# RWKV columns of a hybrid backbone layer: low-rank products ahead of the norm's sums, bonus operands ahead of both directions' work

## The chip, the cores and the metric

The kernel runs on one core of a Trainium2 chip. The metric is the device time of one execution in microseconds (us); lower is better. The engines of the core work side by side, each through its own instructions in order: TensorE (PE, with its weight loads PEld), VectorE (DVE), ScalarE (ACT), GpSimd (POOL), and SyncE (SP), which here only issues DMAs. ACT issues DMAs too.

## The reference, cut to what matters

One layer of a diffusion backbone over 256 context and 2048 latent tokens (2304 in all). After a modulated norm, one input projection feeds two head groups; the change lies in the preparation of the second, eight heads of two-directional RWKV-7 mixing with 64 channels each:

```python
u = _dwconv(z[..., 3 * ATT_WIDTH:], w_ts)          # width-3 shift over tokens
r, kr, v = ...                                     # 512 columns of u each
xw, xa, xg = ...                                   # 2x64, 2x64 and 128 columns
w_log = -softplus(-(w0 + einsum('btnl,nlc->btnc', tanh(xw), w2))) - 0.5
decay = exp(-exp(w_log))
a = sigmoid(a0 + einsum('btnl,nlc->btnc', xa, a2))
g = sigmoid(xg) @ g2
kk = heads(kr * k_k)
kk = kk * rsqrt(sum(kk * kk, -1) + 1e-12)          # the norm, per head
kd = kr[:, :, None] * (1.0 + (a - 1.0) * k_a)      # per direction
S_f, y_f = _wkv_scan(..., kk, kk * a_f, v, kd_f); S_b, y_b = _wkv_scan(..., kk, kk * a_b, v, kd_b, reverse)
y = groupnorm(y_f + y_b) * ln_g + ln_b
bonus = sum(sum(r * kd * r_k, -1) * v, directions)
out = (y + bonus) * g
```

Attention, the output projection, the gated MLP with its convolution and the final norm follow; the change doesn't touch them.

## The kernel before, in words

The program runs in stages: the input projection with attention's columns, then `rwkv_columns`, then attention, the scan, the output projection and the MLP. This case is about `rwkv_columns`.

Tokens go in three blocks of 768 (b = 2, 1, 0). In a block, three projections make the inputs of the low-rank products (`lora`), and then each of four head pairs p (128 columns, two heads) takes three: `kr`, `r` and `v`. A projection is one `gemm`: 48 matmuls (line 55) over eight chunks of the model width, three terms of high and low parts, two halves of columns in two PSUM tiles `g`. `conv3` (lines 114 and 116) takes a pair of such tiles out of PSUM: ACT writes the middle tap, DVE adds the two others. There are two tiles of each name `g`, so a gemm waits for the `conv3` of the gemm two ahead of it. For each gemm, ACT rounds a weight tile to its high part (`wh`, line 36), and POOL subtracts it for the low part (`wl`, line 46).

What is left of a pair is the generator `rest`. Its steps run during the *next* pair's three gemms: `gemm3` calls `tick` after each of the eight chunks, so 24 steps are there. Each `yield` ends a step. In order of `rest`:

- the squares of `kr` and their parts `sh`, `sl` (ACT squares and rounds, DVE subtracts, line 46);
- **the norm**: per half of the tokens a product of `bones` (ones for each head) with `sh` and `sl` (line 823), its root on ACT (line 841), then on DVE the reciprocal (line 843) and `kk` (line 844);
- **eight low-rank products** of three matmuls (line 823), for two directions, two kinds (`w2`, `a2`) and two halves; each is followed by a Tanh on ACT (line 853), each whole tile by a scale on DVE (line 855);
- `v` transposed, and sent out;
- `ms` (ACT, line 871), the bonus weights `t0` (DVE, lines 874, 876, 877);
- **the directions**: for each a scan over the decay's logarithm (DVE, line 883), two exponentials on ACT (lines 886 and 888), and products that make `ar` and `bk`: on POOL `a` times `kk`, `kr` times `m`, `r` times `e1` (lines 892, 895, 898), on DVE lines 893, 896 and 897. `ar` and `bk` have one buffer each and leave by DMA (line 900);
- **the bonus operands** `th`, `tl`, the high and low part of `t0`, in the buffers `sh` and `sl` (ACT line 36, DVE line 46), then an empty step;
- the bonus's product of `bones` with `th` and `tl`, which DVE multiplies by `v` (line 913), and the gate's product (ACT line 916, DVE line 917), per half. All products share three PSUM tiles `lr`.

The order written here is not quite the order on an engine: a scheduler ahead of the compiler sorts each engine's instructions by its own estimates, within what the data allow. So the rows of each engine's order are shown below where they matter. When the last pair's rest has run out, attention begins; its loads stand behind the last `g` writes (line 921) in SP's queue.

Of the kernel before, what the change touches and what calls it, by code (L numbers as in the profile page):

```python
# [7 lines left out]
F32 = mybir.dt.float32  # L8
F32R = mybir.dt.float32r
BF16 = mybir.dt.bfloat16  # L10
F16 = mybir.dt.float16
AF = mybir.ActivationFunctionType
ALU = mybir.AluOpType
# [9 lines left out]
BLK = 768  # L23
# [19 lines left out]
def split(hi_eng, lo_eng, hi, lo, src):  # L43

    copy(hi_eng, hi, src)
    lo_eng.tensor_sub(lo, src, hi)  # L46
# [761 lines left out]
def rwkv_columns(tc, ident, consts, R, h, window, gemm):  # L808


    nc = tc.nc
    with tc.tile_pool(name="i1", bufs=1) as i1, tc.tile_pool(name="i2", bufs=2) as i2, tc.tile_pool(
        name="ip", bufs=2, space=PSUM
# [4 lines left out]
        def product(st, x, s):  # L818

            ps = ip.tile([128, 512], F32, name="lr", bufs=3)  # L820
            terms = [(st[0], x[0]), (st[1], x[0]), (st[0], x[1])] if len(st) == 2 else [(st[0], x[0]), (st[0], x[1])]
            for i, (A, B) in enumerate(terms):
                nc.tensor.matmul(ps[:, :384], A, B[:, s], start=i == 0, stop=i == len(terms) - 1)
            return ps[:, :384]

        HALVES = [slice(q * 384, q * 384 + 384) for q in range(2)]

        def rest(b, p, kr, r, v, lora):
# [4 lines left out]
            sh = i2.tile([128, BLK], F32R, name="sh", bufs=1)  # L833
            sl = i2.tile([128, BLK], F32R, name="sl", bufs=1)
            split(nc.scalar, nc.vector, sh, sl, sq)
            for _ in range(3):
                yield
            kk = i2.tile([128, BLK], F32, name="kk", bufs=1)
            nrm = i2.tile([128, BLK], F32, name="sq", bufs=1)
            for s in HALVES:  # L840
                nc.scalar.activation(nrm[:, s], product((bones,), (sh, sl), s), AF.Sqrt, bias=tiny)
                yield
            nc.vector.reciprocal(nrm, nrm)
            nc.vector.scalar_tensor_tensor(kk, kr, col["k_k"][:, pc], nrm, op0=ALU.mult, op1=ALU.mult)
            lr = []
            for n in range(2):
                rows = slice(n * 64, n * 64 + 64)
                for w, x, bias in (("w2", lora[0], col[f"w0{n}"]), ("a2", lora[1], col[f"a0{n}"])):

                    t = i2.tile([128, BLK], F32, name=w)  # L850
                    for s in HALVES:
                        ps = product([z[rows, p, :] for z in lw[w]], [z[rows] for z in x], s)
                        nc.scalar.activation(t[:, s], ps, AF.Tanh, scale=0.5, bias=bias[:, pc])
                        yield
                    nc.vector.tensor_scalar(t, t, 0.5, 0.5, op0=ALU.mult, op1=ALU.add)
                    lr.append(t)
            vt = i2.tile([128, 6, 128], F32, name="vt", bufs=1)
            for t in range(0, 6, 3):
                tp = ip.tile([128, 512], F32, name="aux", bufs=1)
# [15 lines left out]
            mm = i2.tile([128, BLK], F32, name="sl", bufs=1)  # L875
            nc.vector.tensor_add(mm, ms[0], ms[1])
            nc.vector.tensor_mul(t0, t0, mm)
            for n in range(2):
                sg, a = lr[2 * n : 2 * n + 2]
                m = ms[n]  # L880
                cs = i2.tile([128, BLK], F32, name="t1")
                rev = (lambda t: t) if n == 0 else (lambda t: t[:, ::-1])
                nc.vector.tensor_tensor_scan(rev(cs), rev(cmask[n]), rev(sg), 0.0, ALU.mult, ALU.add)
                e1 = decay[n]
                lo = 1 - n
                nc.scalar.activation(e1[:, :, lo : lo + 64], ch(cs), AF.Exp, scale=-CW)
                e2 = i2.tile([128, BLK], F32, name="e2", bufs=1)
                nc.scalar.activation(e2, cs, AF.Exp, scale=CW)
                nc.gpsimd.tensor_copy(R["pc"][:, n, b * 12 : b * 12 + 12, p], e1[:, :, 64 * (1 - n)])
                ar = i2.tile([128, 12, 2, 64], F32, name="ar", bufs=1)  # L890
                bk = i2.tile([128, 12, 2, 64], F32, name="bk", bufs=1)
                nc.gpsimd.tensor_mul(a, kk, a)
                nc.vector.scalar_tensor_tensor(bk[:, :, 0, :], ch(a), -1.0, ch(e2), op0=ALU.mult, op1=ALU.mult)
                kd = i2.tile([128, BLK], F32, name="t1")
                nc.gpsimd.tensor_mul(kd, kr, m)
                nc.vector.tensor_mul(bk[:, :, 1, :], ch(kd), ch(e2))
                nc.vector.tensor_mul(ar[:, :, 0, :], ch(kk), e1[:, :, n : n + 64])
                nc.gpsimd.tensor_mul(ar[:, :, 1, :], ch(r), e1[:, :, lo : lo + 64])
                for nm, t in (("ar", ar), ("bk", bk)):
                    nc.sync.dma_start(  # L900
                        R[nm][n, b * 12 : b * 12 + 12, :, p, :].rearrange("c p s -> p c s"),
                        t.rearrange("p c x t -> p c (x t)"),
                    )
                yield
            th = i2.tile([128, BLK], F32R, name="sh", bufs=1)
            tl = i2.tile([128, BLK], F32R, name="sl", bufs=1)
            split(nc.scalar, nc.vector, th, tl, t0)
            yield
            yield
            g1 = i2.tile([128, BLK], F32, name="m0", bufs=1)  # L910
            g2 = i2.tile([128, BLK], F32, name="m1", bufs=1)
            for s in HALVES:
# [661 lines left out]
```

## Time and profile before

| | us |
|---|---|
| median of 3 runs (4527.21 to 4528.01) | 4527.84 |
| profiled execution, its time | 4528.56 |
| profiled execution, its span | 4526.8 |
| PE busy, share of the span | 3852.0, 85% |
| DVE busy | 3115.0, 69% |
| POOL busy | 2323.6, 51% |
| ACT busy | 1845.9, 41% |

The span is the time from the first to the last instruction of the profiled execution. Busy shares are means over all stages; `rwkv_columns` takes some 620 us of the span, from about 560 to 1180 us, and is read by itself below.

### The profile page before, as it was taken

Reading aid. Unit: us, or ns where it says so; the run is one execution under the profiler, and the core shown is the slowest. Engines: PE = TensorE matmul, PEld = TensorE weight load, DVE = VectorE, ACT = ScalarE, POOL = GpSimd, SP = SyncE. Lnnn points to the kernel's source line nnn. Section 1 sums busy time; section 2 is a strip of 40 time slices with the busy share of each in tenths; the row PEclk is TensorE's granted clock in tenths of the full one; section 3 lists DMA queues with packets and bytes.
Section 4 is the critical chain, followed back from the end, with each engine's and each line's share of the span. In section 5 each row is a group of like instructions: output and inputs, shape, how many; then the busy total and the mean of one; then the engine's idle time right before and its main releaser. Section 6 shows DMA issues by size and latency. Waiting matters only on the chain. (4 is left out here: it accounts for less than half of the span.)

```text
span 4526.8 us, 78134 instructions
## 1 busy us (share of the span) xinstructions
PE 3852.0 (85%) x29954; PEld 3414.9 (75%) x29954; DVE 3115.0 (69%) x4658; ACT 1845.9 (41%) x3728; POOL 2323.6 (51%) x1879
## 2 busy tenths in 40 slices
PE   6798987888388887899886886999988999889996
PEld 6787877777266666788775665888877999779995
DVE  4325586868577774566664224888888888878887
ACT  2421254544377773455442223333334333343332
POOL 0334344545234336555664444666656776667662
PEclk9899998989599997999998997999988999999998
DMA  5787545453756623323343443221223222232222
GB/s 211 243 280 212 145 117 165 114 159 112 178 116 135 128 58 102 86 76 81 95 102 105 167 149 94 61 66 61 66 80 112 68 64 70 84 106 63 70 70 66
DMA packets 682387, 513.24 MB, mean 113 GB/s; under 512 B 234691, under 2 KB 612612, under 8 KB 677916
## 3 DMA queue, kind: packets, MB, share of 16 engines
q1 hardware_dynamic: 508444, 378.64, 30.0%
q10 hardware_dynamic: 170080, 118.06, 8.8%
q0 software_dynamic: 3488, 11.54, 0.8%
q8 instruction: 236, 3.87, 0.4%
q14 instruction: 139, 1.14, 0.1%
HBM read 369.85 MB, written 139.76 MB: 113 GB/s over the span
## 5 line engine op out<-in xcount | busy, mean ns | idle before, releaser
L46 POOL TENSOR_TENSOR wl<-wr,wh 128x512 fp32r<-128x512 f32 (+1 forms) x349 | 613.2, 1758 | 575.3 <-ACT wh L36 503.8
L55 PE MATMUL g<-h,wh 128*128 128x384 f32 (+1 forms) x2592 | 641.8, 359 | 32.3 <-DVE r L116 8.4
L36 ACT ACTIVATE wh<-wr 128x512 fp32r<-128x512 f32 (+1 forms) x485 | 336.3, 704 | 500.2 <-DMA wr<-in_w_ffn_dram 210.1
L55 PEld LDWEIGHTS g<-h,wh 128*128 128x128 f32 x2592 | 487.6, 200 | 67.1 <-issue 27.7
L507 DVE TENSOR_TENSOR yacc<-yacc,yp 128x512 f32<-128x512 f32 x756 | 479.3, 680 | 28.9 <-PE yp L499 5.2
L456 PE MATMUL u<-hT,wh 128*128 128x386 f32 x1056 | 366.8, 347 | 38.3 <-DVE st L465 24.8
L456 PE MATMUL u<-lT,wh 128*128 128x386 f32 x1056 | 364.4, 345 | 12.2 <-DVE lT L46 12.2
L456 PE MATMUL u<-hT,wl 128*128 128x386 f32 x1056 | 364.4, 345 | 3.8 <-POOL wl L46 3.8
L55 PE MATMUL g<-h,wl 128*128 128x384 f32 (+1 forms) x1296 | 359.9, 355 | 0.0
L499 PE MATMUL yp<-w2h,gh 128*128 128x512 f32 x792 | 273.1, 418 | 48.6 <-DVE yacc L507 20.0
L46 DVE TENSOR_TENSOR wl<-wr,wh 128x512 fp32r<-128x512 f32 (+1 forms) x136 | 251.9, 1853 | 63.2 <-ACT wh L36 63.1
L456 PE MATMUL u<-h,wh 128*128 128x386 f32 x792 | 272.7, 344 | 19.3 <-ACT h L36 17.5
L456 PE MATMUL u<-l,wh 128*128 128x386 f32 x792 | 271.7, 345 | 8.2 <-DVE l L46 7.9
L456 PE MATMUL u<-h,wl 128*128 128x386 f32 x792 | 274.4, 346 | 0.0
L499 PE MATMUL yp<-w2l,gh 128*128 128x512 f32 x792 | 257.8, 404 | 0.0
L499 PE MATMUL yp<-w2h,gl 128*128 128x512 f32 x792 | 257.0, 403 | 0.0
L55 PEld LDWEIGHTS g<-h,wl 128*128 128x128 f32 x1296 | 250.8, 200 | 2.8 <-issue 2.5
L456 PEld LDWEIGHTS u<-hT,wh 128*128 128x128 f32 x1056 | 203.0, 192 | 51.8 <-DVE st L465 31.9
L499 PEld LDWEIGHTS yp<-w2h,gh 128*128 128x128 f32 x792 | 151.6, 193 | 108.9 <-DVE yacc L507 50.1
L354 POOL TENSOR_TENSOR s<-wr 128x512 f32<-128x512 f32 x66 | 85.8, 1300 | 271.3 <-DMA wr<-in_w_ffn_dram 271.3
L456 PEld LDWEIGHTS u<-lT,wh 128*128 128x128 f32 x1056 | 203.4, 193 | 17.8 <-DVE lT L46 17.5
L1273 DVE TENSOR_TENSOR X<-iv,mmask 128x256 f16<-128x256 f32 x360 | 146.3, 422 | 98.7 <-PE iv L1270 93.8
(333 smaller groups left out, 10085.3 us busy)
## 6 DMA issues: line engine op xcount, KB each, us to landing
wr<-in_w_ffn_dram SPq DMA_DIRECT2D x198, 512.0 KB
wr<-in_w_in_dram ACTq DMA_DIRECT2D x45, 512.0 KB
wr<-in_w_in_dram ACTq DMA_DIRECT2D x72, 256.0 KB
d_ar<-ar SPq DMA_DIRECT2D x24, 768.0 KB
d_bk<-bk SPq DMA_DIRECT2D x24, 768.0 KB
kd<-d_ks SPq DMA_DIRECT2D x32, 576.0 KB
bk<-d_bk SPq DMA_DIRECT2D x72, 256.0 KB
ar<-d_ar SPq DMA_DIRECT2D x288, 64.0 KB
```

The lines of the kernel that those rows point to most:

```text
L36: eng.activation(dst, src, AF.Copy, scale=1.0 if scale is None else scale)
L46: lo_eng.tensor_sub(lo, src, hi)
L55: nc.tensor.matmul(ps[q][:, : e - a], A[:, c, :], B[c][:, a:e], start=c == 0 and n == 0, stop=c == KT - 1 and n == 2)
L354: nc.gpsimd.tensor_sub(s3, a11, a21)
L456: nc.tensor.matmul(acc[q], A[a][x][:, c, :], T[t][c][y], start=i < 3 and c == 0 and n == 0, stop=c == KH - 1 and n == 2, skip_group_check= ...
L499: nc.tensor.matmul(yps[q], A[:, t * 128 : t * 128 + 128], B[:, q * 512 : q * 512 + 512], start=n == 0, stop=n == 2)
L507: nc.vector.tensor_add(d, d, yps[q])
L1273: nc.vector.tensor_mul(half(X1, n), X, mk)
```

## The change

The edit is confined to the order of steps in `rest`. No arithmetic, shape, engine or buffer count changes. The eight low-rank products come straight behind the squares, in the steps that were empty or held the norm, and the norm comes behind them. The bonus operands `th`, `tl` are split as soon as `t0` is there, ahead of both directions, and each direction is followed by two yields. The edit, with the parts that are only moved cut to "...":

```diff
             split(nc.scalar, nc.vector, sh, sl, sq)
-            for _ in range(3):
-                yield
+            yield
+            lr = []
+            for n in range(2):
+                rows = slice(n * 64, n * 64 + 64)
+                for w, x, bias in (("w2", lora[0], col[f"w0{n}"]), ("a2", lora[1], col[f"a0{n}"])):
+                    t = i2.tile([128, BLK], F32, name=w)
+                    for s in HALVES:
+                        ps = product([z[rows, p, :] for z in lw[w]], [z[rows] for z in x], s)
+                        nc.scalar.activation(t[:, s], ps, AF.Tanh, scale=0.5, bias=bias[:, pc])
+                        yield
+                    nc.vector.tensor_scalar(t, t, 0.5, 0.5, op0=ALU.mult, op1=ALU.add)
+                    lr.append(t)
             kk = i2.tile([128, BLK], F32, name="kk", bufs=1)
             ...
             nc.vector.scalar_tensor_tensor(kk, kr, col["k_k"][:, pc], nrm, op0=ALU.mult, op1=ALU.mult)
-            lr = []
-            ...
             nc.vector.tensor_mul(t0, t0, mm)
+            th = i2.tile([128, BLK], F32R, name="sh", bufs=1)
+            tl = i2.tile([128, BLK], F32R, name="sl", bufs=1)
+            split(nc.scalar, nc.vector, th, tl, t0)
+            yield
             for n in range(2):
                 ...
                 yield
-            th = i2.tile([128, BLK], F32R, name="sh", bufs=1)
-            tl = i2.tile([128, BLK], F32R, name="sl", bufs=1)
-            split(nc.scalar, nc.vector, th, tl, t0)
-            yield
-            yield
+                yield
```

In the changed kernel the lines shift: the reciprocal is line 854, `kk` 855, the scale 847, the scan 886, `t0` 873, 875 and 876, the directions' products on DVE 896, 899 and 900, the bonus 912.

**DVE from the norm's reciprocal to the bonus operand**, pair 1 of block 2 (the rest that runs during pair 2's gemms). In a row stand the line, the operation, output and inputs. Before, 23 instructions follow the reciprocal up to the bonus operand `sl<-sq,sh`; these are the last 12:

```order
L876 TENSOR_TENSOR sl<-m_5017,m_5019 128x768
L897 TENSOR_TENSOR ar<-kk,e_4084 128x12x64
L877 TENSOR_TENSOR sq<-sq,sl 128x768
L893 SCALAR_TENSOR_TENSOR bk<-a_4905,e_5029 128x12x64
L896 TENSOR_TENSOR bk<-t_5036,e_5029 128x12x64
L883 SCALAR_TENSOR_TENSOR t_5049<-zones,w_4945 128x768
L116 SCALAR_TENSOR_TENSOR r<-g_4936,cols,r 128x385
L116 SCALAR_TENSOR_TENSOR r<-g_4937,cols,r 128x383
L116 SCALAR_TENSOR_TENSOR r<-g_4936,cols,r 128x383
L897 TENSOR_TENSOR ar<-kk,e_4085 128x12x64
L116 SCALAR_TENSOR_TENSOR r<-g_4937,cols,r 128x384
L46 TENSOR_TENSOR sl<-sq,sh 128x768
```

The 11 ahead of these, behind the reciprocal, are a scale, `kk`, four of `kr`'s `conv3`, three scales, `t0` and the first scan. In the changed kernel, the whole way from the reciprocal to the same operand is:

```order
L854 RECIPROCAL sq<-sq 128x768
L875 TENSOR_TENSOR sl<-m_5005,m_5007 128x768
L855 SCALAR_TENSOR_TENSOR kk<-kr,cols,sq 128x768
L116 SCALAR_TENSOR_TENSOR r<-g_4948,cols,r 128x385
L873 SCALAR_TENSOR_TENSOR sq<-r,cols,kr 128x768
L896 SCALAR_TENSOR_TENSOR bk<-a_4869,e_5027 128x12x64
L876 TENSOR_TENSOR sq<-sq,sl 128x768
L900 TENSOR_TENSOR ar<-kk,e_4084 128x12x64
L116 SCALAR_TENSOR_TENSOR r<-g_4949,cols,r 128x383
L46 TENSOR_TENSOR sl<-sq,sh 128x768
```

Both scans, the four scales, `kr`'s `conv3`, one product of `bk`, one of `ar` and two instructions of `r`'s `conv3` no longer stand between the two.

**DVE ahead of the reciprocal**, the same pair of the changed kernel, from the norm's own operand `sl` on:

```order
L46 TENSOR_TENSOR sl<-sq,sh 128x768
L847 TENSOR_SCALAR w_4845<-w_4845 128x768
L886 SCALAR_TENSOR_TENSOR t_5024<-zones,w_4845 128x768
L847 TENSOR_SCALAR a_4869<-a_4869 128x768
L899 TENSOR_TENSOR bk<-t_5034,e_5027 128x12x64
L847 TENSOR_SCALAR w_4893<-w_4893 128x768
L886 SCALAR_TENSOR_TENSOR t_5053<-zones,w_4893 128x768
L847 TENSOR_SCALAR a_4917<-a_4917 128x768
L116 SCALAR_TENSOR_TENSOR kr<-g_4837,cols,kr 128x385
```

Behind the last come three more of `kr`'s `conv3` and then the reciprocal. Before, the reciprocal was the instruction right behind `sl`; the scans, the scales and the first direction's product with `kd` have moved ahead of it.

**PE around the norm** of the same pair, in the changed kernel:

```order
L823 MATMUL lr<-lora_4222,l_a_2786 128x384
L55 MATMUL g_4948<-h_2885,wh 128x386
L55 MATMUL g_4949<-h_2885,wh 128x384
L55 MATMUL g_4948<-h_2885,wl 128x386
L55 MATMUL g_4949<-h_2885,wl 128x384
L55 MATMUL g_4948<-h_2887,wh 128x386
L55 MATMUL g_4949<-h_2887,wh 128x384
L823 MATMUL lr<-sh,bones 128x384
L823 MATMUL lr<-sl,bones 128x384
```

The last low-rank matmul stands ahead of the norm, and the norm's first product lies behind the first chunk of the second gemm (`r`). Before, it lay in the first gemm (`kr`), ahead of the low-rank products but for one to three matmuls. Counted in the same order for the first pairs of block 2: from the norm's last matmul to the bonus's product with `sl` there are now 70 to 78 gemm matmuls, three of the gate's product and six transposes (before 107 to 116 gemm matmuls, and 21 to 24 low-rank ones besides); from there to the next norm's last matmul there are 71 to 74 gemm matmuls, three of the gate's and all 24 low-rank ones (before 32 to 34 gemm matmuls, three of the gate's, one to three low-rank ones). In all engines, the order outside this stage is that of before.

## Rows read from the trace of the kernel before

**Rows 1.** The page's first line.
```profile
span 4526.8 us, 78134 instructions
```

**Rows 2.** Waits of PE between 500 and 1200 us: total us, times, longest.
```profile
PE lr L823 <- ACT sh L36: 53.0, 10, 14.6
PE lr L823 <- DVE sl L46: 36.6, 11, 6.3
```

**Rows 3.** Windows between reciprocals: length, busy us of PE, PEld, DVE, ACT, POOL; clock.
```profile
566.95:611.65 44.70, 38.39 (x190) 33.35 (x189) 38.44 (x35) 23.43 (x35) 23.64 (x11) 0.92 0.50 133
...
660.68:711.68 51.00, 41.96 (x198) 37.02 (x198) 39.07 (x35) 21.94 (x33) 22.40 (x10) 0.90 0.56 180
711.68:785.20 73.52, 59.17 (x306) 55.90 (x305) 47.77 (x48) 33.91 (x50) 39.77 (x18) 0.88 0.51 137
...
933.21:1007.22 74.01, 62.49 (x310) 58.77 (x309) 47.51 (x61) 33.81 (x50) 40.47 (x18) 0.86 0.47 127
...
1103.44:1150.09 46.65, 35.85 (x156) 28.70 (x156) 40.17 (x43) 22.75 (x36) 14.99 (x8) 0.82 0.33 102
sum 583.14, PE 486.94 PEld 430.18 DVE 453.85 ACT 276.55 POOL 284.06; mean PE 44.27 PEld 39.11 DVE 41.26 ACT 25.14 POOL 25.82
```

**Rows 4.** Timeline of PE: start, duration, instructions, idle before them.
```profile
565.64 0.79 PE L823 MATMUL lr<-lora,l_w 64*128 64x384 f32 x3
...
567.62 0.79 PE L823 MATMUL lr<-lora,l_w 64*128 64x384 f32 x3
...
600.50 1.01 PE L823 MATMUL lr<-sl,bones 128*128 128x384 f32 x2 [6.31 <-DVE sl L46]
...
601.95 1.49 PE L55 MATMUL g<-h,wh 128*128 128x386 f32 x4
603.23 0.85 PE L55 MATMUL g<-h,wl 128*128 128x386 f32 x2
...
606.80 0.86 PE L55 MATMUL g<-h,wh 128*128 128x386 f32 x4
607.50 0.34 PE L55 MATMUL g<-h,wl 128*128 128x386 f32 x1
```

**Rows 5.** Timeline of DVE, from one pair's reciprocal to its bonus operand.
```profile
611.65 4.95 DVE L843 RECIPROCAL sq<-sq 128x768 f32<-128x768 f32 x1 [3.01 <-ACT sq L841]
...
616.94 1.00 DVE L844 SCALAR_TENSOR_TENSOR kk<-kr,cols,sq 128x768 f32<-128x768 f32 x1
618.75 2.19 DVE L116 SCALAR_TENSOR_TENSOR kr<-g,cols,kr 128x385 f32<-128x385 f32 x4 [0.81 <-ACT kr L114]
...
633.47 2.57 DVE L877 TENSOR_TENSOR sq<-sq,sl 128x768 f32<-128x768 f32 x1
635.96 0.95 DVE L893 SCALAR_TENSOR_TENSOR bk<-a,e 128x768 f32<-128x768 f32 x1
...
639.19 3.95 DVE L883 TENSOR_TENSOR_SCAN t<-zones,w 128x768 f32<-128x768 f32 x1
...
646.02 2.05 DVE L46 TENSOR_TENSOR sl<-sq,sh 128x768 fp32r<-128x768 f32 x1
```

**Rows 6.** Timeline of POOL beside the rows of DVE above.
```profile
632.69 2.53 POOL L892 TENSOR_TENSOR a<-kk,a 128x768 f32<-128x768 f32 x1
...
650.13 2.38 POOL L46 TENSOR_TENSOR wl<-wr,wh 128x1024 fp32r<-128x1024 f32 x1 [2.87 <-ACT wh L36]
```

**Rows 7.** Timeline of POOL and DVE around a wait for `ar`.
```profile
737.35 2.38 POOL L898 TENSOR_TENSOR ar<-r,e 128x768 f32<-128x768 f32 x1
...
744.07 2.87 DVE L897 TENSOR_TENSOR ar<-kk,e 128x768 f32<-128x768 f32 x1 [1.86 <-DMA d_ar<-ar]
```

**Rows 8.** Timeline of PE and DVE at the stage's end.
```profile
1136.02 0.52 PE L55 MATMUL g<-h,wh 128*128 128x384 f32 x1
...
1179.55 0.61 DVE L917 SCALAR_TENSOR_TENSOR m<-m,cols,lr 128x384 f32<-128x384 f32 x1
```

More of the change, by code (lines that the diff above doesn't have):

```diff
@@ L835, in rest @@
             split(nc.scalar, nc.vector, sh, sl, sq)
-            for _ in range(3):
-                yield
[L838 to L841, printed above, removed]
-                yield
-            nc.vector.reciprocal(nrm, nrm)
-            nc.vector.scalar_tensor_tensor(kk, kr, col["k_k"][:, pc], nrm, op0=ALU.mult, op1=ALU.mult)
+            yield
             lr = []
@@ L856, in rest @@
                     lr.append(t)
+            kk = i2.tile([128, BLK], F32, name="kk", bufs=1)
+            nrm = i2.tile([128, BLK], F32, name="sq", bufs=1)
+            for s in HALVES:
+                nc.scalar.activation(nrm[:, s], product((bones,), (sh, sl), s), AF.Sqrt, bias=tiny)
+                yield
+            nc.vector.reciprocal(nrm, nrm)
+            nc.vector.scalar_tensor_tensor(kk, kr, col["k_k"][:, pc], nrm, op0=ALU.mult, op1=ALU.mult)
             vt = i2.tile([128, 6, 128], F32, name="vt", bufs=1)
@@ L904, in rest @@
                 yield
-            th = i2.tile([128, BLK], F32R, name="sh", bufs=1)
-            tl = i2.tile([128, BLK], F32R, name="sl", bufs=1)
-            split(nc.scalar, nc.vector, th, tl, t0)
-            yield
-            yield
+                yield
             g1 = i2.tile([128, BLK], F32, name="m0", bufs=1)
```

## The prediction, made before the changed kernel was run

> **What bounds the kernel now.** I looked at the waits of PE in the stage first, since its gemms are the stage's largest work. Two rows stand out, both of the products with `bones`: 53.0 us waiting for ACT's `sh` and 36.6 us for DVE's `sl` [rows 2]. These buffers serve the norm and the bonus, so the question is which of the two waits. The timeline answers: the 6.31 us at 600.50 [rows 4] lie 11 us ahead of a reciprocal [rows 5], and by PE's order that place is the bonus's of the pair before; the long ones in other pairs stand at the same place. So PE waits for the bonus operands, and the norm's products hardly wait.
>
> Why are they late? DVE's timeline shows one chain in program order: the reciprocal starts at 611.65, and the bonus operand `sl` ends at 646.02 + 2.05 = 648.07 [rows 5], 36.4 us later, with scales, scans, `conv3` and the directions' products between. DVE had itself idled 3.01 us for the norm's root ahead of that reciprocal [rows 5]. This is a loop: reciprocal, DVE's chain, bonus product on PE, the PE work up to the next norm, next reciprocal. Its period can be read from the windows: the nine gaps inside blocks make (144.73 + 148.01 + 142.87) / 9 = 48.4 us, from the starts and ends in [rows 3]. DVE is busy for (453.85 - 47.77 - 47.51) / 9 = 39.8 us of each, the sum less the two long gaps [rows 3]. It is the second bound, not far below.
>
> What would PE need if nothing made it wait? A gemm matmul takes (607.50 - 606.80) / 4 = 0.175 us at the full clock, a low-rank product of three (567.62 - 565.64) - 6 x 0.175 = 0.93 us, since a step also holds six gemm matmuls [rows 4]. A pair has 144 and 8 of these: 25.2 + 7.4 us; the norm's and bonus's eight matmuls, the gate's six and six transposes I put at 0.18 us each, an estimate from the gemm row: 3.6 us. **PE alone: 36.2 us** for a pair, 12.2 below the period. Part of that is clock: behind the wait at 600.50 four matmuls take (603.23 - 601.95) = 1.28 us, 0.32 each [rows 4], the lower of the two levels (1.2 and 2.4 GHz), after PE had idled; at 606.80 it is back. A pace of 0.32 instead of 0.175 over some 4 us of work costs about 2 us for each such wait.
>
> **The change, step by step.** No instruction is added or removed, so only the loop's two halves have to be costed.
>
> First half, reciprocal to `sl`. In the changed order DVE does: reciprocal 4.95, `kk` 1.00, and at the unhindered 0.95 each the sum of `ms`, `t0`, one `bk`, the product with the sum, one `ar`, the operand itself [rows 5]; two parts of `conv3` at 2.19 / 4 = 0.55 [rows 5] (four in the next pair). 4.95 + 1.00 + 6 x 0.95 + 2 x 0.55 = 12.8 us, 13.9 with four. To this come waits: `bk` needs POOL's `a` times `kk`, which starts when `kk` ends and takes 2.53 us [rows 6], against 1.5 us of `conv3` and `t0`: 1.0 us. Lowest: 13.8. Upper bound: four of the six at the hindered 2.57 us, as the product with the sum in [rows 5], makes 13.9 + 1.0 + 4 x 1.62 = 21.4. Much of POOL's work on the directions has moved ahead of the reciprocal as well, so I take the middle, **17.5 us**, for 36.4 before. The root from PE's last norm matmul to the reciprocal adds about 1 us, an estimate: one wait of PE's end, one ACT instruction.
>
> PE needs for the same stretch 70 to 78 gemm matmuls, three of the gate's, six transposes and four with `bones`: 83 to 91 at 0.175 makes 14.5 to 15.9 us. So the bonus product will still wait: 18.5 - 15 = **3.5 us**, and the clock will still fall behind it, 2 us.
>
> Second half, `sl` to the next norm's end: 71 to 74 gemm matmuls, three of the gate's, four of the norm's: 78 to 81 at 0.175, 13.9 us, and eight low-rank products at 0.93, 7.4: **21.3 us**. The norm lies six chunks later than before, and that lengthens this half: before, 32 to 34 gemm matmuls and the rest made some 8 us. The order thus takes 19 us out of one half and puts 13 into the other, which is why the gain is smaller than the wait.
>
> Period: 1 + 17.5 + 21.3 + 2 = 41.8 us. DVE's own load of 39.8 leaves it 2 us of air, with a start of the reciprocal that waits for the root besides; I add 1.2 us for that, an estimate between nothing and the 3.01 us that it idled there: **43.0 us**. Nine gaps: 9 x (48.4 - 43.0) = 48.6 us.
>
> The two gaps with a new block's low-rank projections are 73.5 and 74.0 us [rows 3]. PE alone would need 36.2 + 144 x 0.175 = 61.4. There too the bonus waits; its PE cover is only some 60 matmuls, 11 us, so I keep 18.5 - 11 = 7.5 and 2 of clock: 70.9, and 2 x 2.8 = 5.6 us.
>
> The end: from the last gemm matmul at 1136.5 to the last result at 1180.2 [rows 8] 43.6 us pass without a gemm to hide anything. The eight low-rank products now come first, but the root's way is as long; three scales leave the DVE chain behind the reciprocal. Three of 0.95 at most: I take 2 us, and bounds of 0 and 5.
>
> Sum: 48.6 + 5.6 + 2 = 56 us. The profiled execution took 4528.56 for a span of 4526.8 [rows 1], 0.7 above the median of 4527.84, so the difference holds for both: 4527.8 - 56 = **4472 us**.
>
> What hides the moved work: the scans, scales and `kd`'s product run while PE makes the low-rank products, where DVE idled for the root (3.01 us [rows 5]) or worked on what now follows. If that cover is gone, they delay the reciprocal itself, and with it all of the loop. That is the second rival. The bonus operands use the norm's buffers `sh` and `sl`, which PE has read by then in both orders. SP's and POOL's queues pass no new wait but that `ar` and `bk` leave closer together (third rival).
>
> **Rivals.** (a) *The bonus wait vanishes.* If POOL hinders DVE little, the first half is 13.8 + 1 us, just PE's 15, no clock is lost, and DVE's load becomes the bound: 39.8 us. Nine times 8.6 is 77; the two long gaps fall by up to 8 each, the end by 5: 4528 - 98 = 4430. For it: DVE's rows at 0.95. Against it: the hindered ones are as common.
>
> (b) *POOL takes it back; slower.* The row at 633.47 takes 2.57 us and ends at 636.04, 0.8 us behind POOL's `a` (632.69 + 2.53 = 635.22), and the `bk` behind it takes 0.95 [rows 5, 6]: DVE waited out POOL's instruction. The scan at 639.19 took 3.95 [rows 5]. Now both scans, the `kd` product, four scales and the norm's `sl` stand ahead of the reciprocal, next to POOL's weight parts (2.38 us [rows 6]), two `kd` and two `ar`. If each of eight or so of these waits out one of POOL's, some 1.6 us, DVE's work of 39.8 - 17.5 = 22.3 us in the second half grows by up to 13 to 35. The point that decides is 48.4 - 18.5 = 29.9 us: beyond it a pair takes longer than before. At 31.5 us the period is 50, and nine pairs lose 14: 4542. The Trainium skill, SBUF — State Buffer, section "SBUF: two separate sides", says the same in general: a VectorE instruction with two SBUF inputs and a GpSimd one lock each other out for a whole instruction. By that, the trace agrees with 2.57 for 0.95; but the lock's total is that of the same instructions as before, and it would only cost if DVE had less free time than it needs, where 48.4 - 39.8 = 8.6 us are free now.
>
> (c) *The single buffers of `ar` and `bk`.* POOL's `ar` ended at 737.35 + 2.38 = 739.73, and the next `ar` could be written at 744.07, after a wait of 1.86 us for the DMA [rows 7]: 4.3 us from end to free. The two directions lie some 5 us apart now, instead of more than 8. If DVE stops there for 2 to 3 us in each pair ahead of the bonus's multiplication, the gate's product on PE waits for a `lr` tile, and half of the gain goes: 4528 - 26 = 4502.
>
> (d) *No change*, since the scheduler's order or DVE's load pins the period at 48: 4528.
>
> **How the numbers follow.** My forecast, with its own range of 4452 to 4492, has 0.52; (a) 0.17, (c) 0.14, (b) 0.10, (d) 0.07. What a measurement of this kernel tells from no change is about 0.2%, 9 us. Faster: 0.52 + 0.17 + 0.14 = 0.83; same 0.07; slower 0.10. The range from 4430 to 4515 leaves out (b), (d) and a little of (a).
>
> **What would show it.** In the changed profile: gaps between reciprocals of 42 to 44 us inside blocks; 15 to 20 us from the reciprocal to the bonus's `sl`, for 36.4; PE's waits for `sh` and `sl` together at about half of the 89.6 us; the scans starting ahead of the reciprocal. I am wrong in mechanism if the gaps stay above 47, if DVE's idle time ahead of the reciprocal is gone and the reciprocal starts more than 3 us behind PE's last norm matmul (b), or if DVE or POOL wait for `d_ar` or `d_bk` in most pairs (c). I am wrong in size if the waits vanish altogether.

## The result, and the profile after

The changed kernel took 4502.91 us (median of 4 runs, 4502.51 to 4504.22) beside 4527.52 us for the kernel before on the same chip: ratio 0.9948, 95% interval 0.9933 to 0.9963. That is 24.6 us less. The forecast was 4472 us, 56 us less. The sign is right, but less than half of the gain came: the time lies outside the forecast's own range of 4452 to 4492 us and only inside the wide one of 4430 to 4515. The profiled execution took 4502.95 us.

Two lines answer to [rows 1] and [rows 2]: the page's first line, and the waits of PE between 500 and 1200 us.

```profile
span 4501.1 us, 78132 instructions
```

```profile
PE lr L823 <- ACT sh L36: 61.6, 12, 16.1
...
PE lr L823 <- DVE sl L46: 13.2, 7, 5.1
```

The waits for the two operands fell from 89.6 to 74.8 us, not to the half that was forecast. The windows between reciprocals (columns as in [rows 3]) say where the rest sits:

```profile
622.09:664.74 42.65, 38.66 (x191) 34.24 (x189) 36.86 (x37) 24.20 (x36) 20.24 (x12) 0.92 0.49 139
664.74:715.47 50.73, 44.67 (x225) 40.01 (x224) 32.39 (x34) 19.85 (x31) 16.40 (x7) 0.93 0.65 215
715.47:789.51 74.04, 59.66 (x302) 54.15 (x300) 53.03 (x50) 36.37 (x52) 40.34 (x21) 0.88 0.45 116
...
875.99:928.88 52.89, 44.49 (x221) 39.31 (x220) 33.03 (x37) 19.99 (x31) 16.38 (x7) 0.94 0.64 206
928.88:1006.60 77.72, 59.99 (x297) 54.33 (x296) 53.13 (x62) 36.35 (x53) 39.08 (x21) 0.85 0.41 104
...
sum 543.44, PE 464.66 PEld 414.14 DVE 426.82 ACT 269.93 POOL 244.43; mean PE 42.24 PEld 37.65 DVE 38.80 ACT 24.54 POOL 22.22
```

The first two gaps of each block took 43.05 us on average, where 43.0 was forecast. The gap that ends a block (50.73 and 52.89 us) and the long one behind it (74.04 and 77.72) did not shrink at all: before, they took 51.00 and 51.35, 73.52 and 74.01 us.

DVE's timeline inside a block, which answers to [rows 5]:

```profile
622.09 4.94 DVE L854 RECIPROCAL sq<-sq 128x768 f32<-128x768 f32 x1
...
627.75 3.16 DVE L855 SCALAR_TENSOR_TENSOR kk<-kr,cols,sq 128x768 f32<-128x768 f32 x1
...
631.37 2.28 DVE L873 SCALAR_TENSOR_TENSOR sq<-r,cols,kr 128x768 f32<-128x768 f32 x1
633.57 2.56 DVE L896 SCALAR_TENSOR_TENSOR bk<-a,e 128x768 f32<-128x768 f32 x1
636.05 0.94 DVE L876 TENSOR_TENSOR sq<-sq,sl 128x768 f32<-128x768 f32 x1
...
638.32 0.94 DVE L46 TENSOR_TENSOR sl<-sq,sh 128x768 fp32r<-128x768 f32 x1
```

From the reciprocal to the end of `sl` 638.32 + 0.94 - 622.09 = 17.2 us pass, 17.5 were forecast, 36.4 it was. Three instructions (`kk`, the product of `r` and `kr`, and `bk`) still take 2.3 to 3.2 us, where 0.95 to 1.00 us is the time of the same without a neighbour on POOL.

At the block's end the timelines of ACT, DVE and POOL look otherwise:

```profile
688.44 0.33 ACTq L559 DMA_DIRECT2D h<-d_hlo  x1
...
699.39 0.33 ACTq L559 DMA_DIRECT2D h<-d_hlo  x1
699.77 1.05 ACT L845 ACTIVATE w<-lr,cols 128x384 f32<-128x384 f32 x2 [10.75 <-DMA h<-d_hlo]
```

```profile
700.85 0.56 DVE L847 TENSOR_SCALAR w<-w 128x768 f32<-128x768 f32 x1 [8.75 <-ACT w L845]
...
721.76 2.60 DVE L875 TENSOR_TENSOR sl<-m,m 128x768 f32<-128x768 f32 x1
724.29 2.55 DVE L873 SCALAR_TENSOR_TENSOR sq<-r,cols,kr 128x768 f32<-128x768 f32 x1
...
735.49 2.55 DVE L46 TENSOR_TENSOR sl<-sq,sh 128x768 fp32r<-128x768 f32 x1
```

```profile
723.50 2.52 POOL L895 TENSOR_TENSOR a<-kk,a 128x768 f32<-128x768 f32 x1
...
734.71 2.51 POOL L898 TENSOR_TENSOR t<-kr,m 128x768 f32<-128x768 f32 x1
```

ScalarE's own queue issues the loads of the next block's window (`h`, line 559) one by one over 11 us. The kernel has nine buffers for the eight chunks of each part of `h`, so these loads must wait until the block's last gemm has read a chunk. The first low-rank Tanh behind them starts after an idle time of 10.75 us, and DVE's scale with it. Then nearly every DVE instruction of that pair's chain lies beside one of POOL: 738.04 - 715.47 = 22.6 us to the end of `sl`. Both became theories to test.

### The profile page after: what moved, and what is told of

Its sections match the earlier page's. It is cut to its first block, busy times and chain, and to the rows that moved or that the text cites. A ratio compares the mean times of both kernels' runs of the same rounds, so it can differ in the third digit from the quotient of the medians.

```text
span 4501.1 us, 78132 instructions
## 1 busy us (share of the span) xinstructions
PE 3836.3 (85%) x29954; PEld 3399.2 (76%) x29954; DVE 3097.7 (69%) x4658; ACT 1846.5 (41%) x3728; POOL 2282.8 (51%) x1879
## 5 line engine op out<-in xcount | busy, mean ns | idle before, releaser
L456 PE MATMUL u<-hT,wh 128*128 128x386 f32 x1056 | 367.1, 348 | 38.5 <-DVE st L465 25.8
```

Of the source, the lines that this page charges most:

```text
L456: nc.tensor.matmul(acc[q], A[a][x][:, c, :], T[t][c][y], start=i < 3 and c == 0 and n == 0, stop=c == KH - 1 and n == 2, skip_group_check= ...
```

## The experiments

The kernels were run in four sets (E1 to E4, E5 to E8, E9 to E12, E13 to E16), each on another chip. The kernel before took 4525 to 4530 us as the median beside each set, so kernels are compared by their ratios to it. "Inside" is the mean of the first two gaps of each block, "end" the mean sum of the two gaps that end a block, "chain" the mean stretch from the reciprocal to the end of `sl` in the first two pairs of each block. All three are read from the starts and ends of the instructions in the timelines, so they are those of one profiled execution; those of E3, E5, E8 and E16 hold gaps at a low clock, of which more below. E7, E9, E10, E12, E13 and E14 leave terms of the reference out and only measure.

| kernel | us | ratio to before (95%) | inside | end | chain |
|---|---|---|---|---|---|
| before | 4527.5 | 1 | 47.8 | 124.9 | 35.9 |
| changed | 4502.9 | 0.9948 (0.9933 to 0.9963) | 43.1 | 127.7 | 18.1 |
| E1 low-rank first only | 4502.1 | 0.9939 (0.9924 to 0.9955) | 42.7 | 129.1 | 17.9 |
| E2 bonus first only | 4510.6 | 0.9959 (0.9943 to 0.9974) | 45.4 | 125.4 | 30.1 |
| E3 changed, loads on SyncE | 4468.3 | 0.9869 (0.9850 to 0.9888) | 44.3 | 115.8 | 17.9 |
| E4 before, loads on SyncE | 4506.5 | 0.9944 (0.9923 to 0.9965) | 47.1 | 118.7 | 35.3 |
| E5 bonus ahead of the norm | 4510.0 | 0.9968 (0.9950 to 0.9987) | 46.0 | 124.4 | |
| E6 own buffers | 4507.1 | 0.9947 (0.9932 to 0.9962) | 43.4 | 131.7 | 15.2 |
| E7 changed, no POOL products | 4449.4 | 0.9821 (0.9807 to 0.9836) | 40.6 | 114.0 | 16.8 |
| E8 E5 and loads on SyncE | 4488.6 | 0.9906 (0.9879 to 0.9933) | 46.7 | 113.9 | |
| E9 E7 and loads on SyncE | 4418.4 | 0.9774 (0.9753 to 0.9794) | 40.2 | 108.5 | 16.6 |
| E10 before, no POOL products | 4437.7 | 0.9807 (0.9793 to 0.9822) | 39.1 | 118.8 | 27.2 |
| E11 E3 and kd on DVE | 4465.7 | 0.9872 (0.9857 to 0.9886) | 43.5 | 114.5 | 18.6 |
| E12 E10 and loads on SyncE | 4418.6 | 0.9763 (0.9747 to 0.9780) | 38.5 | 112.0 | 26.5 |
| E13 changed, idle POOL products | 4525.4 | 0.9995 (0.9985 to 1.0005) | 46.3 | 130.2 | 21.3 |
| E14 before, idle POOL products | 4532.0 | 1.0005 (0.9996 to 1.0015) | 46.6 | 129.7 | 33.9 |
| E15 E4, kd and a on DVE | 4479.4 | 0.9897 (0.9883 to 0.9912) | 45.4 | 114.3 | 36.1 |
| E16 E3, kd and a on DVE | 4516.9 | 0.9966 (0.9942 to 0.9990) | 53.1 | 115.6 | 15.6 |

### E1 and E2: one part of the change alone

E1 takes the changed kernel and puts the split back behind both directions (diff below); E2 takes the kernel before and moves only the split, the other way:

```
...
-            split(nc.scalar, nc.vector, th, tl, t0)
-            yield
             for n in range(2):
...
-                yield
...
+            split(nc.scalar, nc.vector, th, tl, t0)
+            yield
+            yield
```

> The low-rank products stand ahead of the norm's sums, as in the changed kernel, but the bonus operands are split behind both directions' work, as before the change. Theory (loop of two halves): the second half keeps its 21.3 us, since the norm lies late; the first half, reciprocal to the bonus's sl, holds the directions' remaining bk and ar products again, five more instructions of 0.95 to 2.5 us than the 18.5 us of the changed kernel, so about 25 us; with 1 us for the root and 2 us of lost clock the period is 49 us, against 47.8 before: no gain or a loss, 4530 us (4515 to 4550). Rival (the low-rank products ahead of the norm are what brings the gain, by themselves): gaps of 43 to 44 us, 4505 us or less.

> The norm's sums come first, three chunks into the pair, and the low-rank products behind them, as before the change, but the bonus operands are split ahead of both directions' work. Theory (loop of two halves): the first half now holds eight low-rank products and eight chunks of gemm, 8 x (6 x 0.175 + 0.93) = 15.8 us, then the scales, the sum of ms, the product and sl, with three other DVE instructions between: about 27 us from reciprocal to sl, with 24 us of PE work as its cover, so PE waits little; the second half is short, some 16 us by DVE's own instructions. Period 44 us, so 9 x (47.8 - 44) = 34 us less than before: 4493 us (4475 to 4515). Rival (DVE has no air: it idles under the low-rank products and its 39.8 us of work come on top): period 47 us, 4520 us. Rival (both halves fit under PE): period 40 us, 4455 us.

E1 is as fast as the changed kernel, so its rival holds. DVE's timeline shows why the edit could not test the theory:

```profile
618.53 4.94 DVE L854 RECIPROCAL sq<-sq 128x768 f32<-128x768 f32 x1
...
634.77 0.94 DVE L46 TENSOR_TENSOR sl<-sq,sh 128x768 fp32r<-128x768 f32 x1
```

The split stands 16.24 us behind the reciprocal, as in the changed kernel (16.23): once the low-rank products lie ahead of the norm, the scheduler puts the split there by itself. Inside the first block both programs have DVE's instructions in the same order; in the second a few neighbours are swapped. The second part of the change thus does nothing beside the first. Alone (E2) it brings 19 us by its median, with a chain of 30.1 us where about 27 were expected, and a time 17 us above the expected one.

### E3 and E4: the window loads on another queue

```
-        def window(b, cols=(0, WIN)):
+        def window(b, cols=(0, WIN), eng=nc.scalar):
...
-                h = window(b)
+                h = window(b, eng=nc.sync)
```

> The changed kernel, with the window loads of the last two blocks issued by SyncE's queue instead of ScalarE's. Theory (at the block's end ScalarE's queue stands behind window loads that wait for a free h buffer, and the low-rank products' Tanh stands behind them): Tanh no longer waits 10.75 us there, the gap that ends a block falls from 50.7 and 52.9 us towards 43, and the long gaps by some 3 us each, so 10 to 20 us less than the changed kernel: 4488 us. Rival (the hindrance of DVE by POOL in the block's last pair, or PE's own order with the norm behind 91 gemm matmuls, costs the boundary): the gaps stay within 2 us, 4503 us.

> The kernel before the change, with the same two window loads on SyncE's queue. Theory: before, the same loads held the norm's root, and DVE idled 8.84 us ahead of the reciprocal at 711.68; the gaps that end a block, 51.0 and 51.35 us, fall to the 47.8 us of the others, and the long ones by a little: 5 to 10 us less, 4520 us; so the boundary's cost is one that the kernel before had as well, and the change alone could not lift it. Rival (nothing hangs on the loads): 4527 us.

The gain is larger than expected: the changed kernel falls to 0.9869, the one before to 0.9944. In E3's trace the Tanh has no wait to speak of, and the gap that ends the block is now shorter than those inside it (ACT's timeline, then a window between reciprocals):

```profile
690.20 0.58 ACT L845 ACTIVATE w<-lr,cols 128x384 f32<-128x384 f32 x1 [0.17 <-PE lr L823]
```

```profile
664.98:701.99 37.01, 33.17 (x169) 30.24 (x168) 32.04 (x30) 19.79 (x30) 17.81 (x9) 0.91 0.78 234
```

The two gaps of a block's end fall by 127.7 - 115.8 = 11.9 us in the changed kernel and by 6.2 in the one before; 8.6 and 10.6 us more come ahead of the first reciprocal (569.58 for 578.16 us, 556.31 for 566.95). Part of these last is scatter: in five runs of the new order with the loads on ScalarE it lies between 572.7 and 580.0 us, in four of the old between 560.9 and 567.0. So ScalarE's queue cost both kernels time, and the changed one 5.7 us more at each of two ends. With it out of the way the change is worth 4506.5 - 4468.3 = 38 us instead of 25. On the kernel before, the move alone is worth as much as the change alone (0.9944 and 0.9948).

### E5, E6 and E8: the bonus operands cut loose from the norm

```
-            nrm = i2.tile([128, BLK], F32, name="sq", bufs=1)
+            nrm = kk
...
-            th = i2.tile([128, BLK], F32R, name="sh", bufs=1)
-            tl = i2.tile([128, BLK], F32R, name="sl", bufs=1)
+            th = i2.tile([128, BLK], F32R, name="th", bufs=1)
+            tl = i2.tile([128, BLK], F32R, name="tl", bufs=1)
```

`mm` goes into `tl`'s buffer too; that is E6. In E5 and E8 the lines from `ms` to this split stand ahead of the norm's products as well, three steps ahead; E8 has the loads on SyncE besides.

> The changed kernel with the bonus operands cut loose from the norm: they get buffers of their own (th, tl; the root goes into kk's buffer and becomes kk in place), and the sum of ms, the product and the split stand ahead of the norm's products, three chunks of gemm apart. Nothing that PE waits for then hangs on the reciprocal. Theory (the loop reciprocal, DVE's chain, bonus product, next norm sets the 43.05 us): PE's waits of 2.7 to 5 us at the bonus and the low clock behind them go, the period falls to 38 to 40 us, the larger of PE's 36.2 and DVE's 37.85 us of work; nine or so gaps of 3 to 5 us: about 35 us less than the changed kernel, 4468 us. Rival (DVE is the bound already, since its few idle microseconds can't be filled): gaps of 41 to 42 us, 4490 us. Rival (the bonus wait is not on the path): 4503 us.

> The changed kernel with the same buffers of their own for the bonus operands, but the program's order left alone. The scheduler then puts one of the chain's instructions, the product of r and kr, ahead of the reciprocal. Theory (loop): the first half is shorter by that instruction, 0.95 to 2.3 us, and by what it had to wait for POOL, so PE's bonus wait falls by 1 to 3 us in each gap: 4485 us (4475 to 4495). Rival (sharing the norm's buffers costs nothing): 4503 us.

> The bonus ahead of the norm with its own buffers, and the window loads of the last two blocks on SyncE's queue. Theory (the loop inside the block and ScalarE's queue at its end are two separate costs): the gains add, 35 us of the one and 35 us of the other, 4432 us. Rival (they share the time at the block's end): 4450 us.

E6 changes nothing (0.9947), where 4485 us were expected, though its chain is 2.9 us shorter. E5 refutes my theory that the loop through the bonus wait holds the changed kernel's period. Waits of PE between 500 and 1200 us, and three windows between reciprocals:

```profile
PE g L55 <- DVE kr L116: 28.8, 2, 14.6
...
PE lr L823 <- ACT th L36: 11.7, 1, 11.7
...
PE lr L823 <- DVE tl L46: 5.7, 4, 3.2
```

```profile
791.20:834.30 43.10, 38.31 (x189) 33.32 (x190) 39.55 (x36) 22.83 (x35) 21.29 (x10) 0.95 0.49 138
834.30:874.80 40.50, 38.76 (x187) 34.05 (x187) 38.79 (x35) 22.95 (x33) 23.08 (x12) 0.93 0.53 153
...
997.50:1053.70 56.20, 51.31 (x194) 42.58 (x192) 40.81 (x44) 24.03 (x36) 21.36 (x10) 0.73 0.38 106
```

PE's wait for the two pairs of operands is mostly gone (17.4 us for 74.8), and the kernel is no faster; 28.8 us for `kr` have come in its place. The gaps at a high clock (45.2 and 39.9 in the first block, 43.1 and 40.5 in the second) make 42.2 us on average, and DVE is busy for 38.8 to 39.6 us of the two shown: behind the bonus wait DVE's load stood nearly at the same mark. The last block's two gaps ran at a clock of 0.73 and 0.70, of which more below. They cost 56.22 + 51.22 - 2 x 42.2 = 23 us, so without the low clock this execution would lie near 4482 us, an estimate; that and the gaps of 42.2 us fit the first rival (gaps of 41 to 42 us, 4490 us). E8 missed both its theory and its rival: at 4488.6 us it is 20 us slower than E3 by the medians, and three of its gaps ran at a clock of 0.67 to 0.74.

### E7, E10, E9 and E12: POOL's products left out

```
-                nc.gpsimd.tensor_mul(a, kk, a)
...
-                nc.gpsimd.tensor_mul(kd, kr, m)
-                nc.vector.tensor_mul(bk[:, :, 1, :], ch(kd), ch(e2))
...
+                nc.vector.tensor_mul(bk[:, :, 1, :], ch(kr), ch(e2))
...
-                nc.gpsimd.tensor_mul(ar[:, :, 1, :], ch(r), e1[:, :, lo : lo + 64])
+                nc.scalar.activation(ar[:, :, 1, :], ch(r), AF.Copy, scale=0.1)
```

So `bk` is made of `a` and `kr` as they are (with another factor for `a`), and ACT writes the second half of `ar` from `r` alone. POOL keeps the weight parts.

> The changed kernel without the directions' six POOL products of a pair: a times kk and kr times m are left out, and the second half of ar is written by ACT as a scaled copy of r (the directions' results are then other ones). POOL keeps the weight parts. Theory (DVE's two-input instructions wait out POOL's, 2.3 to 3.2 us instead of 0.95): four or five instructions of the first half get 1.3 to 2.2 us shorter each, reciprocal to sl falls from 17.2 to 12 or 13 us, below PE's cover of 14.5 to 15.9, the bonus wait and its lost clock go, and the third gaps of the blocks, where nearly every DVE instruction took 2.55 us, fall as well: periods of 37 us, some 45 to 60 us less than the changed kernel, 4452 us. Rival (POOL's products cost DVE time that it has to spare, and the boundary is ScalarE's queue alone): gaps of 41 us or more, 4485 us.

> The kernel before the change without the directions' six POOL products of a pair (left out in the same way). Theory (POOL's products hinder the old order as much as the new one, since its long chain from the reciprocal to sl holds most of them): it falls by about 45 us to 4485 us, and the change would be worth some 35 us without them, not the 56 of the forecast. Rival (the new order pays for POOL what the old one did not, which is what ate half of the forecast's gain): it falls by less than 20 us, to 4510 us or more, and the change would be worth 60 us without them.

> The changed kernel, both without the directions' six POOL products of a pair (left out as in the run without them) and with the window loads of the last two blocks on SyncE's queue. Theory (two separate costs at the block's end: ScalarE's queue, 35 us, and DVE behind POOL, 54 us): the gains add up, 4415 us. Rival (both shorten the same wait): little more than the larger one, 4440 us.

> The kernel before the change, both without the six POOL products and with the window loads on SyncE's queue. Theory (the two costs lie on the old order as on the new one): 4465 us, so that the change would be worth about 50 us where neither is in its way, close to the forecast. Rival (the loop's own gain is limited by PE in the changed kernel): the difference stays at 40 us or less, 4455 us or below.

E7 came out as expected (4449 for 4452 us), and E9 shows that the two costs nearly add (4418 for 4415 us). E10 is the surprise: the kernel before falls by 0.0193, some 87 us, to or below E7. Without POOL's products **the change is worth nothing**: 0.9821 against 0.9807, and 0.9774 against 0.9763 with the loads on SyncE, the intervals overlapping. My theory for E10 (a fall of 45 us) was far off, and its rival farther; that for E12 (4465 us) missed by 46 us, and its rival (4455 us or below) holds. DVE's timeline in E10:

```profile
598.09 4.95 DVE L843 RECIPROCAL sq<-sq 128x768 f32<-128x768 f32 x1 [2.00 <-ACT sq L841]
...
618.05 0.95 DVE L877 TENSOR_TENSOR sq<-sq,sl 128x768 f32<-128x768 f32 x1
...
624.33 0.95 DVE L46 TENSOR_TENSOR sl<-sq,sh 128x768 fp32r<-128x768 f32 x1
```

In the old order, 624.33 + 0.95 - 598.09 = 27.2 us from the reciprocal to `sl`, where it took 36.4 with POOL's products [rows 5]; its gaps inside a block take 39.1 us.

### E13 and E14: POOL's products into a buffer that nothing reads

E7 and E10 get these lines besides:

```
+                scr = i2.tile([128, BLK], F32, name="scr", bufs=1)
+                nc.gpsimd.tensor_mul(scr, kk, a)
+                nc.gpsimd.tensor_mul(scr, kr, m)
...
+                nc.gpsimd.tensor_mul(ch(scr), ch(r), e1[:, :, lo : lo + 64])
```

> The changed kernel with the directions computed as in the runs without POOL's products (left out of the results in the same way), but POOL still does the six multiplications of a pair, on the same operands, into a buffer that nothing reads. So POOL's work is back and nobody waits for its results. Theory (while POOL multiplies, DVE's two-input instructions stand still, so the hindrance itself costs the time): 4500 us, nearly all of the 54 us comes back. Rival (what cost was the wait for POOL's results, bk for a and for kd): 4450 us, as without the products.

> The kernel before the change in the same way: POOL does the six multiplications of a pair into a buffer that nothing reads, and the directions are computed without them. Theory (hindrance): most of the 88 us comes back, 4515 us, with a chain from the reciprocal to sl of 34 us or more instead of 27. Rival (waits for POOL's results): 4440 us.

Everything that E7 and E10 had won is lost again, though nothing uses the results of POOL's products. DVE's groups of the product with the sum of `ms`, between 560 and 1150 us (busy us, mean ns), in E10 and then in E14:

```profile
L877 DVE TENSOR_TENSOR sq<-sq,sl 128x768 f32<-128x768 f32 x12 | 11.4, 947 | 0.1
```

```profile
L877 DVE TENSOR_TENSOR sq<-sq,sl 128x768 f32<-128x768 f32 x11 | 22.8, 2076 | 0.1
```

So the cost is the hindrance, not a wait for results: the same instruction takes 947 ns alone and 2076 ns on average with POOL's products back. This agrees with the Trainium skill, SBUF — State Buffer, section "SBUF: two separate sides", by which a VectorE instruction with two SBUF inputs and a GpSimd instruction that reads SBUF exclude each other for a whole instruction.

The whole stage says the same. These are the stretches from the first reciprocal to the last in E10, E14, E7 and E13, with the columns of [rows 3]:

```profile
560.86:1070.13 509.27, 465.02 (x2338) 410.67 (x2337) 378.76 (x444) 291.84 (x425) 123.56 (x64) 0.95 0.54 153
565.52:1148.05 582.53, 482.55 (x2338) 426.36 (x2337) 463.01 (x444) 292.94 (x425) 277.80 (x130) 0.90 0.47 134
579.97:1078.73 498.76, 457.50 (x2293) 405.46 (x2291) 379.78 (x435) 285.37 (x417) 116.18 (x62) 0.94 0.54 154
573.84:1147.28 573.44, 478.09 (x2293) 423.29 (x2291) 452.31 (x436) 284.30 (x417) 273.47 (x128) 0.88 0.46 134
```

DVE's work is the same in a pair of rows but for the hindrance. Its busy time grows by 84.3 us in E14 and the stage by 73.3; in E13 they grow by 72.5 and 74.7. For the two kernels of the case, against E10 and E7, they are 75.1 and 73.9 us before, 47.0 and 44.7 us changed. So the change took 75.1 - 47.0 = 28 us of hindrance off DVE.

E14 is the clean one of the pair: DVE and ACT wait for POOL 2.9 and 32.4 us in the stage, and ACT 27.8 us in E10. In E13 they wait 6.7 and 41.1 us, where ACT alone waits 3.6 us in E7, so waits may have a share there. E13 is even slower than the changed kernel, with a chain of 21.3 us for 18.1. POOL's rows show a difference: the product of `kr` and `m`, in the changed kernel and then in E13, where the reciprocals start at 622.09 and 617.66:

```profile
622.94 1.84 POOL L898 TENSOR_TENSOR t<-kr,m 128x768 f32<-128x768 f32 x1 [6.58 <-ACT m L870]
```

```profile
629.95 2.52 POOL L897 TENSOR_TENSOR scr<-kr,m 128x768 f32<-128x768 f32 x1
```

In the changed kernel it lies ahead of the reciprocal or beside it in most gaps inside blocks, and the reciprocal, with one input, still takes 4.94 us. In E13, with the one buffer `scr`, POOL's products come in the program's order, behind `kk`, and this one starts 9 to 23 us behind the reciprocal in every pair, beside the chain. So E13 is another placement of the same work, which DVE pays for with 72.5 us instead of 47.0. Between E14 and E13 the change is worth next to nothing too (1.0005 and 0.9995, the intervals overlapping).

### E11, E15 and E16: products moved from POOL to DVE

```
-                nc.gpsimd.tensor_mul(kd, kr, m)
+                nc.vector.tensor_mul(kd, kr, m)
```

E15 and E16 move `a` in the same way.

> The changed kernel with the window loads on SyncE's queue, and kr times m moved from POOL to DVE for both directions. Theory (a POOL product costs DVE more by holding up its neighbour, 1.3 to 2.2 us, and by DVE's wait of 4.3 us for it, than the 0.95 us that it takes on DVE itself): 5 to 15 us less than with the loads alone, 4458 us. Rival (DVE's load is what binds, so 1.9 us more of it per pair make the stage longer): 4485 us.

> The kernel before the change with the window loads on SyncE's queue and four of the six POOL products of a pair (a times kk, kr times m) on DVE. Theory (without POOL's products the old order is as fast as the new one, 4418 us for both with the loads on SyncE, so with two of six left it gets most of that back, less 12 pairs of 3.8 us more DVE work): 4465 us. Rival (DVE's load binds the old order at once): 4500 us.

> The changed kernel in the same way, loads on SyncE's queue and four of the six products on DVE. Theory: with kd alone on DVE it took 4465.7 us; two more products of 0.95 us on DVE for two of 2.4 us less on POOL change little, 4465 us. Rival (the shorter way from the reciprocal to sl, without POOL's a in it, takes the bonus wait away): 4445 us.

E11 is level with E3 (0.9872 and 0.9869), where 5 to 15 us were expected; I take it that DVE's own work takes what POOL gives back, which is argued and not shown. E15 gains on E4 (0.9897 for 0.9944, some 21 us), 14 us short of what was expected. E16 is slower than E3, against both its theory and its rival, and scatters from 4478 to 4534 us; its trace shows the low clock described below. **The best kernels that compute the reference are E3 and E11**, some 35 us below the changed one.

## Why the prediction was right in kind and wrong in size

- **The period inside a block** was right: 43.0 us forecast, 43.05 measured; the chain 17.5 forecast, 18.1 on average; the rest of the gap 25.5 with root, clock and reserve, 25.0 measured; PE's wait for the bonus 3.5 forecast, 4.2 on average. That the sum came so close is in part luck: the 1.2 us of reserve was an estimate between two bounds, and it was added because DVE's own load of 39.8 us was taken over from before, while it fell to (426.82 - 53.03 - 53.13) / 9 = 35.6 us. Six such gaps gave 6 x (47.77 - 43.05) = 28.3 us, of 32.4 forecast.
- **The step that failed: "Nine gaps: 9 x (48.4 - 43.0) = 48.6 us", and with it "two long gaps ... 5.6 us".** The gaps that end a block were counted as any other. They and the long ones were to bring 2 x 5.4 + 5.6 = 16.4 us and lost 5.5: 21.9 us missing. What [rows 3] gave as a mean of 48.4 hid that a block's last gap has other things in it. E3 and E4 show one: ScalarE's queue stands behind window loads, which costs the new order 11.9 us at each end and the old one 6.2, since the low-rank Tanh moved to where the loads are. E7 and E10 show the other: POOL's products cost the new order 127.7 - 114.0 = 13.7 us there, the old one 6.2. With both out of the way (E9, E12) the change takes 112.0 - 108.5 = 3.5 us off each end, of 8.2 forecast.
- **The stage's beginning and end**: the first reciprocal came 11.2 us later, a term that the forecast left out, the last gap was 16.9 us shorter (29.78 for 46.65) and the tail 3.0 us: 8.7 us together, of 5.4 + 2 forecast. All in all the stage ended 31.5 us earlier.
- **Behind the stage** the profiled execution gave back 5.8 us, 3352.5 for 3346.6 us. The other kernels took 3345 to 3356 us there, E1, with the changed kernel's order inside the blocks, 3345: I take it for scatter, which is argued and not shown. So the forecast's 56.2 us lost 32.4 - 28.3 = 4.1 inside blocks, 21.9 at the ends and 5.8 behind the stage, and 1.3 came on top: 25.7 us, the difference of the two spans.
- **The reason given for the gain was half the truth.** I put the chain of 36.4 us (35.9 on average) down to the order alone. E10 shows 35.9 - 27.2 = 8.7 us of it to go with POOL's products, E7 only 18.1 - 16.8 = 1.3 us of the new one. Without these products the order takes 27.2 - 16.8 = 10.4 us out of the first half and puts (40.6 - 16.8) - (39.1 - 27.2) = 11.9 into the second: nothing gained (POOL's weight parts still hinder DVE in both). What the change brings is that POOL's products hit DVE less, and above all not in the chain that PE waits for.
- **Rival (b)** had the right mechanism and the wrong side: POOL's hindrance was dearer in the old order. It said that the lock's total would be that of the same instructions; that did not hold (75.1 us before, 47.0 changed), since it depends on what lies beside what. Its sign of being wrong was met in part: DVE's idle time ahead of the reciprocal is 0 to 0.9 us in the changed kernel, but the reciprocal mostly starts 0.8 to 2.4 us behind PE's last norm matmul; only at the two block ends it is 4.0 us. **Rival (a)** falls with E5: with the bonus wait gone the gaps were 42.2 us, not 39.8.
- **Rival (c)**: its time, 4502 us, is the measured one, and its sign was met on POOL. Between 560 and 1150 us of the changed kernel DVE waited only 1.6 us in all for `d_ar` and 0.7 for `d_bk`, but POOL 43.7 us in eight waits, where it was 0.2 before:

```profile
POOL ar L901 <- DMA d_ar<-ar: 43.7, 8, 8.3
```

  The way that (c) named, DVE stopping ahead of the bonus, is out. Behind POOL's stops little is seen to wait: PE never waits for POOL in the stage, DVE 12.0 us for the product of `kr` and `m`, ACT 5.9. In E13 POOL writes no `ar` and never stops for one, and the kernel is not faster, but its POOL work lies elsewhere. So the match of the time looks like chance; what POOL's stops cost by themselves, no run separates. **Rival (d)** is out by the interval.

Open is how much of the loss at a block's end lies in each of the two causes when both are there: alone they explain 2 x 5.7 + 2 x 7.5 = 26.4 us of a loss of 21.9, but with both out of the way (E9, E12) the two ends regain only 2 x (2.8 + 3.5) = 12.6. So they overlap, and the remaining 9.3 us of the loss has no cause shown.

## What to carry to other kernels

Before a mean over repeated gaps is multiplied, read the gaps one by one: the ones at a loop's end hold work of the next round, and a step moved there waits for other things. A long chain on one engine is not due to its order until its instructions have been held against their own shortest time; where the same shape takes 0.95 and 2.5 us, find the neighbour first. DMA issues that wait for buffers belong on a queue with no computing behind them: here that alone was worth as much as the change.

## What the runs showed of the hardware

A short wait of PE can cost far more than the 2 us of the prediction. In E3, PE idled 3.99 us up to 628.31 and 0.71 up to 636.83, and then ran at the lower level while it was busy without a gap (stretches of 10 us; the columns are those of [rows 3]):

```profile
640.00:650.00 10.00, 10.00 (x27) 7.37 (x27) 3.52 (x4) 2.44 (x5) 1.83 (x2) 0.50 0.53 148
650.00:660.00 10.00, 10.00 (x28) 7.38 (x27) 3.79 (x5) 4.00 (x8) 1.82 (x1) 0.50 0.01 2
```

The granted clock is 0.50, so 1.2 GHz, and 27 or 28 matmuls start in 10 us. The changed kernel had a like wait at the same place in its program, and its clock was back at full in the second such stretch:

```profile
640.00:650.00 10.00, 10.00 (x45) 8.75 (x44) 9.82 (x13) 5.60 (x9) 5.58 (x3) 0.83 0.96 281
650.00:660.00 10.00, 10.00 (x47) 7.49 (x46) 5.12 (x7) 5.35 (x9) 3.69 (x3) 1.00 0.49 138
```

In E3 that gap took 52.5 instead of 42.9 us, some 10 us for one episode. E16 has several of them, the first behind waits of 2.03 and 3.80 us, and its executions, with mean clocks from 0.919 to 0.934, differ by 57 us:

```profile
650.00:660.00 10.00, 10.00 (x28) 7.37 (x27) 4.85 (x6) 2.99 (x6) 1.84 (x2) 0.50 0.46 146
660.00:670.00 10.00, 10.00 (x28) 7.38 (x26) 4.41 (x5) 2.95 (x6) 0.00 (x0) 0.50 0.01 2
```

What decides between a short and a long stay at the lower level, no run here shows.
